# Weights stationary for both token blocks, and merged mixer chains, in a two-layer hybrid encoder trunk

## The chip, the cores and the metric

The kernel runs on one core of one Trainium2 chip. The metric is device time in microseconds (us) of one execution. Engines are named as in the profile: PE (TensorE matmul), PEld (its loads of the stationary operand), DVE (VectorE), ACT (ScalarE), POOL (GpSimd), SP (SyncE, which issues the DMAs).

## What is computed

One sequence of 256 tokens of 1024 float32 values goes through two layers. In the reference each layer is:

```python
x = layer_norm(ALPHA * x + 0.5 * swiglu(x, ffn1_w_gu[l], ffn1_w_down[l]), ln1_g[l], ln1_b[l])
h = x @ w_in[l]
dq, dk, dv, mz, mxbc, mdt, gq, gk, gv, gz, gb, ga = jnp.split(h, IN_SPLITS, axis=-1)
a_out = diff_attention_mixer(dq, dk, dv, ...)
m_out = mamba2_mixer(mz, mxbc, mdt, ...)
g_out = gated_deltanet_mixer(gq, gk, gv, gz, gb, ga, ...)
mix = jnp.concatenate([a_out, m_out, g_out], -1) @ w_out[l]
x = layer_norm(ALPHA * x + mix, ln2_g[l], ln2_b[l])
x = layer_norm(ALPHA * x + 0.5 * swiglu(x, ffn2_w_gu[l], ffn2_w_down[l]), ln3_g[l], ln3_b[l])
```

`swiglu` is `(silu(x @ gate) * (x @ up)) @ w_down` with 2816 hidden channels. Mamba's inputs `mxbc` (1024 channels) and DeltaNet's `gq, gk, gv` (768 channels) go through a causal depthwise convolution of four taps and a silu along the tokens. DeltaNet also needs the inverse of a unit lower triangular 128x128 matrix for each of four heads and two blocks of tokens.

## The kernel before

The 256 tokens are two blocks `b` of 128, one token a partition. All large products have float32 operands in two parts (`hi` and `lo`, type float32r), so each is three matmuls: `mm3` (L215) multiplies hi by hi, hi by lo and lo by hi, at L219, L220 and L222 or L226. There the stationary operand is 128 tokens of `x`, transposed, and the moving operand is a weight piece of up to 512 columns; the result has tokens on partitions.

Weights come as a stream of units of 128x1024 values (`load`, L239), split by ACT (hi, L230) and DVE (lo, L231) in two halves each. A unit of the gate and up projection (`gu`) holds two of the eight slices of the inner dimension for 256 gate and 256 up columns; four units make a chunk `c`, and 11 chunks a feed-forward, followed by 22 units of `w_down`. The program is a list of units with a block each (`order`, L1019): block 1 follows block 0 by four to five units, so that one block's norm (`norm`, L338) has the other block's products beside it. `job` (L273) issues the products of one unit and one block into a PSUM tile of 512 columns; each block has two such tiles (`psA`, `psB`) and two `aux` tiles for everything small.

After the last unit of a chunk a chain of small steps (a generator) begins. For `gu` it is `after_gu` (L392): silu on ACT, product on DVE, then `to_parts` (L383): two transposes on PE (`hTps`, L235) and a split, because `w_down` wants the hidden channels on partitions. In the mixers the projections come in groups (`qk`, `v`, `dqk`, `m0`, `m1`, `mz`, `dvz`), and every group starts a chain for its block: `conv` (L411) transposes the group on PE, copies it from PSUM to SBUF (ACT, L420), scales two taps on ACT (L435 to L439) and adds two on DVE (L445); `decays` (L465) makes step sizes and 128x128 decay matrices (`ar` on POOL at L503, `dps` on PE); `after_qk` (L530) is DeltaNet, with the products `ssps`, `laps` and the transposes `ktok`, and with `inverse` (L671): five levels, in each of which DVE transposes `T`, PE makes `gps`, DVE makes `G`, PE makes `ups` and DVE updates `TT`. All small products go through `mm` (L326) on plain float32; the trace shows two matmul instructions for each of them.

The chains are recorded between the products: a chain says how long a step takes, and its next step is recorded once PE has been given that time by a model clock, multiplied by a factor from the table `PACE`. Then a scheduler orders each engine's instructions by readiness and priority, so the order on an engine isn't exactly the order of recording.

Of the kernel before, what the change touches and what calls it, by code (L numbers as in the profile page):

```python
# [27 lines left out]
TAPS = 2  # taps of the convolutions on ScalarE  # L28
SP = 2  # pieces in which a unit of weights is split
WS = 19  # tiles of half a bank for a block of tokens  # L30
LAG = 5  # units between the blocks of tokens: at the ends of a segment, and between them
NEAR = 4
# [3 lines left out]
PACE = {  # L36
    "after_v": (0.25, 1.49),
    "decays": (0.36, 0.48, 0.28, 1.01, 0.39, 0.56),
    "after_qk": (0.33, 0.24, 0.66, 0.33, 0.33, 0.33, 0.23, 0.33, 0.5, 0.2, 0.28, 0.33, 0.33, 0.28, 0.33),
    "after_m0": (0.33, 1.09, 0.78, 0.47, 0.78),  # L40
    "after_m1": (0.29, 0.19, 0.07, 0.14, 0.29, 0.24, 0.29),
    "after_mz": (0.39, 0.58, 0.58, 0.47, 0.58),
    "after_dqk": (0.41, 0.69, 0.27, 0.19, 0.27, 0.19, 0.54, 0.14, 0.41, 0.27),
    "after_dvz": (0.48, 0.71, 1.17, 0.39, 0.28, 1.12),
    "gdn_out": (0.12, 0.19, 0.23, 0.39),
    "norm": (0.28, 0.33),
    "after_gu": (4.67, 2.45, 2.33),
}
ORD = (1, 0, 4, 2, 3, 5, 6)
WORD = (4, 5, 2, 3, 6, 7, 0, 1)  # L50
# [3 lines left out]
# columns of the constants  # L54
# [6 lines left out]
# columns of w_in, in the order in which they are projected  # L61
WIN = (
    ("v", ((2824, 256), (3336, 8), (2304, 8))),
    ("qk", ((2312, 512),)),
    ("m0", ((1280, 512),)),
    ("m1", ((1792, 512),)),
    ("dqk", ((0, 512),)),
    ("mz", ((768, 512),)),
    ("dvz", ((512, 256), (3080, 256))),
# [7 lines left out]
def constants():  # L77
    """Masks, the identity and the rotary tables: they depend on shapes alone."""
# [21 lines left out]
class Kernel:  # L100
    def __init__(self, ctx, tc, a, out):
# [32 lines left out]

    def aux(self, b, name):
        return self.aux_p[b].tile([P, 512], F32, tag="aux", name=self.name(name))

# [1 line left out]
    def setup(self):  # L139
# [12 lines left out]
        self.neghalf = c.tile([P, 8], F32, name="neghalf")  # L152
# [7 lines left out]
    def setup_late(self):  # L160
        """What the mixers need, loaded and prepared behind the first products."""
# [53 lines left out]
    def mm3(self, ps, xh, xl, ws, start, stop):  # L215
        """ps[n] += x.T @ w[n] for the parts (xh, xl) and the list of (wh, wl)."""
# [11 lines left out]
    def split_from(self, src, hi, lo):  # L228
        """hi + lo == src exactly, each with 12 bits of mantissa."""
        self.nc.scalar.copy(hi, src)  # L230
        self.nc.vector.tensor_tensor(lo, src, hi.bitcast(F32), op=ALU.subtract)  # L231

    def transposes(self, srcs, ps):
        for n, t in enumerate(srcs):
            self.nc.tensor.transpose(ps[:, n * P : (n + 1) * P], t, self.ident)  # L235
            self.clock += 0.213

# [1 line left out]
    def load(self, u):  # L239
        nc = self.nc  # L240
        raw = self.raw_p.tile([P, 1024], F32, tag="raw", name=self.name("raw"))
        if u["kind"] in ("gu", "win"):
            width = u["width"]
            t = raw[:, : 2 * width].rearrange("p (k n) -> p k n", k=2)
            at = 0
            k0 = u["part"] * 2 * P
            for c0, n in u["cols"]:
                nc.sync.dma_start(
                    t[:, :, at : at + n], u["w"][k0 : k0 + 2 * P, c0 : c0 + n].rearrange("(k p) n -> p k n", p=P)
                )  # L250
                at += n
            u["n"] = 2 * width
# [14 lines left out]
    def ready(self, u, b):  # L267
        st = self.st[b]
        if u["kind"] in ("gu", "win"):
            return st["xseg"] == u["seg"] and len(st["xT"]) > u["part"] // 2  # L270
        return u["k"] // 2 in st["hT" if u["kind"] == "down" else "mT"]

    def job(self, u, b):  # L273
        """The products of a unit of weights and a block of tokens."""
        st = self.st[b]
        wh, wl = u["wh"], u["wl"]
        if u["kind"] in ("gu", "win"):
            width = u["width"]
            if u["part"] == 0:
                st["ps"] = self.ps_p[b].tile([P, 512], F32, tag="ps", name=self.name("ps"))  # L280
            ps = st["ps"][:, :width]
            for kk in range(2):
                k = u["part"] * 2 + kk
                xh, xl = (t[:, k % 4, :] for t in st["xT"][k // 4])
                s = slice(kk * width, (kk + 1) * width)
                self.mm3([ps], xh, xl, [(wh[:, s], wl[:, s])], k == 0, k == KD - 1)
            if u["part"] == 3:
# [832 lines left out]
```

## Time and profile before

| | |
|---|---|
| median of 3 runs | 1136.46 us (1134.03 to 1136.87) |
| span of the profiled execution | 1134.7 us |
| PE busy | 1108.1 us (98%), 5301 matmul instructions |
| DVE busy | 740.0 us (65%) |
| ACT busy | 590.4 us (52%) |
| DMA | 184.92 MB, 163 GB/s in the mean |

The profiled execution's own time is its span; it lies within the runs' spread, 1.8 us under the median. The span has four feed-forwards and two mixers: the mixers lie at about 200 to 380 us and 757 to 936 us. A matmul's record lasts from its start to the end of its pipeline, so records of consecutive matmuls overlap; what a matmul costs the stream is the distance from its start to the next one's start.

### The profile page before, as it was taken

What the parts mean: (1) busy time and instruction counts of PE and PEld (TensorE: products, weight loads), DVE (VectorE), ACT (ScalarE), POOL (GpSimd) and SP (SyncE); (2) the same over time, 40 slices, a digit from 0 to 9 for tenths busy, and PEclk for the clock granted to TensorE, in tenths of its full rate; (3) what the DMA queues carried; (4) which work ended last, traced back from release to release, by engine and by line L of the source; (5) the groups of instructions that cost most, each with busy time, mean ns of one, the idle gap of its engine ahead of it and who ended that gap; (6) DMA issues with size and microseconds to landing.
All of it is one profiled execution on the core that took longest, in us unless ns stands there. A gap on an engine that the chain in (4) does not pass through costs nothing.

```text
span 1134.7 us, 15487 instructions
## 1 busy us (share of the span) xinstructions
PE 1108.1 (98%) x5301; PEld 896.1 (79%) x5301; DVE 740.0 (65%) x1541; ACT 590.4 (52%) x1250; POOL 86.3 (8%) x123
## 2 busy tenths in 40 slices
PE   7999999999998999999999999999999999999996
PEld 6888888867887888888888888888688878888885
DVE  5565555896778955554575565477867887555545
ACT  5565444773674454554445454449546644555440
POOL 0000000032012100000000000001501120000001
PEclk9999999997999999999999999999989999999999
DMA  8775555631224565555575655555311347555650
GB/s 285 237 221 183 187 185 151 196 119 49 70 85 143 191 203 184 185 185 186 167 230 179 186 185 185 186 154 184 111 38 51 108 142 239 182 184 175 186 165 37
DMA packets 138374, 184.92 MB, mean 163 GB/s; under 512 B 15160, under 2 KB 111800, under 8 KB 138296
## 3 DMA queue, kind: packets, MB, share of 16 engines
q1 hardware_dynamic: 138296, 183.95, 52.2%
q8 instruction: 41, 0.67, 0.2%
q14 instruction: 37, 0.30, 0.1%
HBM read 182.86 MB, written 1.05 MB: 162 GB/s over the span
## 4 chain that ended last, share of the span: by engine, by line
PE 91%; DVE 5%; POOL 2%; ACT 1%; issue 1%; DMA 0%; SPq 0%; POOLq 0%; DVEq 0%; ACTq 0%
PE ps L219 18%; PE ps L220 18%; PE ps L226 16%; PE po L220 8%; PE po L219 8%; PE po L226 7%; PE ups L326 2%; PE ps L222 2%; PE gps L326 2%; PE hTps L235 2%; DVE wl L231 1%; PE scps L326 1%; PE xps L235 1%; POOL rsq L367 1%; PE yps L326 1%
## 5 line engine op out<-in xcount | busy, mean ns | idle before, releaser
L231 DVE TENSOR_TENSOR wl<-raw,wh 128x512 fp32r<-128x512 f32 (+1 forms) x672 | 437.5, 688 | 255.3 <-ACT wh L230 250.5
L230 ACT CAST wh<-raw 128x512 fp32r<-128x512 f32 (+1 forms) x672 | 380.8, 614 | 329.1 <-PE ps L226 186.6
L219 PE MATMUL ps<-wh,xh 128*128 128x512 f32 x928 | 374.8, 405 | 2.9 <-ACT wh L230 2.7
L220 PE MATMUL ps<-wl,xh 128*128 128x512 f32 x928 | 368.5, 397 | 0.0
L226 PE MATMUL ps<-wh,xl 128*128 128x512 f32 (+1 forms) x812 | 322.3, 398 | 0.0
L219 PEld LDWEIGHTS ps<-wh,xh 128*128 128x128 f32 x928 | 176.5, 190 | 39.4 <-ACT wh L230 3.3
L220 PEld LDWEIGHTS ps<-wl,xh 128*128 128x128 f32 x928 | 176.6, 190 | 37.3 <-DVE wl L231 1.8
L226 PEld LDWEIGHTS ps<-wh,xl 128*128 128x128 f32 x812 | 154.6, 190 | 35.0 <-issue 1.3
L219 PE MATMUL po<-wh,hT 128*128 128x512 f32 x352 | 139.1, 395 | 0.0
L220 PE MATMUL po<-wl,hT 128*128 128x512 f32 x352 | 138.2, 393 | 0.0
L226 PE MATMUL po<-wh,hT 128*128 128x512 f32 x336 | 105.6, 394 | 0.0
L220 PEld LDWEIGHTS po<-wl,hT 128*128 128x128 f32 x352 | 66.2, 188 | 14.7
L219 PEld LDWEIGHTS po<-wh,hT 128*128 128x128 f32 x352 | 66.1, 188 | 14.7
L226 PEld LDWEIGHTS po<-wh,hT 128*128 128x128 f32 x336 | 63.1, 188 | 14.0
L365 POOL TENSOR_SCALAR rs<-mv 128x1 f32<-128x1 f32 x12 | 6.5, 538 | 793.9 <-DVE mv L349 793.9
L397 DVE TENSOR_TENSOR hh<-ps,sg 128x256 f32<-128x256 f32 x88 | 37.0, 420 | 43.0 <-ACT sg L395 43.0
L395 ACT ACTIVATE sg<-ps 128x256 f32<-128x256 f32 x88 | 33.9, 385 | 55.0 <-PE ps L222 54.7
L222 PE MATMUL ps<-wh,xl 128*128 128x512 f32 (+1 forms) x116 | 46.0, 397 | 0.0
L230 ACT CAST hT<-hTps 128x256 fp32r<-128x256 f32 x88 | 32.5, 369 | 17.0 <-PE hTps L235 17.0
L231 DVE TENSOR_TENSOR hT<-hTps,hT 128x256 fp32r<-128x256 f32 x88 | 35.1, 420 | 0.1
L235 PE MATMUL hTps<-cst,hh 128*128 128x128 f32 x176 | 34.0, 272 | 0.0
L235 PEld LDWEIGHTS hTps<-cst,hh 128*128 128x128 f32 x176 | 24.6, 140 | 11.8
(247 smaller groups left out, 1008.3 us busy)
## 6 DMA issues: line engine op xcount, KB each, us to landing
raw<-in_ffn_w_gu_dram SPq DMA_DIRECT2D x352, 256.0 KB, 3.2
raw<-in_ffn_w_down_dram SPq DMA_DIRECT2D x88, 512.0 KB, 3.5
raw<-in_w_in_dram SPq DMA_DIRECT2D x40, 512.0 KB, 4.5
raw<-in_w_out_dram SPq DMA_DIRECT2D x16, 512.0 KB, 3.6
raw<-in_w_in_dram SPq DMA_DIRECT2D x24, 256.0 KB, 2.8
g<-in_ln_g_dram SPq DMA_DIRECT2D x6, 512.0 KB, 5.0
b<-in_ln_b_dram SPq DMA_DIRECT2D x6, 512.0 KB, 4.9
x<-in_x_dram SPq DMA_DIRECT2D x4, 256.0 KB, 5.8
```

Of the source, the lines that this page charges most:

```text
L219: mm(p, lhsT=xh, rhs=wh, start=start, stop=False)
L220: mm(p, lhsT=xh, rhs=wl, start=False, stop=False)
L222: mm(p, lhsT=xl, rhs=wh, start=False, stop=True)
L226: mm(p, lhsT=xl, rhs=wh, start=False, stop=False)
L230: self.nc.scalar.copy(hi, src)
L231: self.nc.vector.tensor_tensor(lo, src, hi.bitcast(F32), op=ALU.subtract)
L235: self.nc.tensor.transpose(ps[:, n * P : (n + 1) * P], t, self.ident)
L326: self.nc.tensor.matmul(out, lhsT=lhsT, rhs=rhs, start=start, stop=stop)
L365: nc.gpsimd.tensor_scalar(t, ap, mul, add, op0=ALU.mult, op1=ALU.add)
L367: nc.gpsimd.tensor_tensor(r, t, self.neghalf[:, :n], op=ALU.pow)
L395: nc.scalar.activation(sg, ps[:, 0:256], AF.Silu)
L397: nc.vector.tensor_mul(hh, ps[:, 256:512], sg)
```

## The change

**Products.** For the chunks from the third on (`TSC = 2`) and for the mixers' convolved groups (`qk`, `m0`, `v`, `m1`), a unit is multiplied once for both blocks: the stationary operand is a piece of 128 weight columns, the moving operand is 2x128 tokens, 256 columns, and the result has channels on partitions. A unit with 24 such matmuls (L288 of the new kernel) replaces two times six of 512 columns. The first two chunks, `w_down`, `w_out` and the groups `dqk`, `gd`, `mz`, `gz` stay as they were, with tokens stationary; `dvz` and the 16 columns of gates are cut anew into `gd` and `gz`.

**Feed-forward.** `after_gu2` has silu, product and split for 512 columns at once, without transposes.

**PSUM.** One pool of two tiles of 1024 columns (`ps`) serves all products in place of two times two of 512, and `aux` has four tiles for both blocks.

**Mixers.** `conv` has no transposes, no copy and no halo: its four taps read the group's PSUM tile, two on ACT and two on DVE, over 256 tokens, and write `acc`. `decays`, `after_v`, `after_qk`, `inverse`, `after_m0`, `after_m1` and the second half of `after_mz` run once for both blocks on tiles of twice the width. The products `ar` move from POOL to DVE. The groups' order is now `dqk, gd, qk, m0, v, m1, mz, gz`. The table `PACE` is empty, so every step has the factor 0.39.

**Order of units.** Block 1 follows block 0 only at the ends of a segment (`order`); units for both blocks stand alone between.

```diff
-ORD = (1, 0, 4, 2, 3, 5, 6)
-WORD = (4, 5, 2, 3, 6, 7, 0, 1)
+NBIG, NHALF, NH, NS = 15, 7, 7, 36
+TSC = 2
+PACE = {}
+WORD = (0, 1, 6, 7, 2, 3, 4, 5)
...
-        self.ps_p = [pool("psA", 2, **psum), pool("psB", 2, **psum)]
-        self.aux_p = [pool("auxA", 2, **psum), pool("auxB", 2, **psum)]
+        self.ps_p = pool("ps", 2, **psum)
+        self.aux_p = pool("aux", 4, **psum)
...
+    def ps(self, name):
+        return self.ps_p.tile([P, 1024], F32, tag="ps", name=self.name(name))
...
+            if u["both"]:
+                for i, c0 in enumerate(u["tiles"]):
+                    o = g["ps"][:, 256 * i : 256 * i + 256]
+                    for kk in range(ks):
+                        k = u["part"] * ks + kk
+                        xh, xl = (t[:, :, k % 4, :] for t in self.xT[k // 4])
+                        s = slice(kk * width + c0, kk * width + c0 + P)
...
+                        for n, (a, x) in enumerate(((wh[:, s], xh), (wh[:, s], xl), (wl[:, s], xh))):
+                            self.nc.tensor.matmul(
+                                o, lhsT=a, rhs=x, start=k == 0 and n == 0 and i % 2 == 0, stop=end and n == 2,
+                                skip_group_check=True,
+                            )
...
+                if last:
+                    self.spawn(u["then"](u, g["ps"]))
...
+    def after_gu2(self, u, ps):
+        nc = self.nc
+        p4 = ps.rearrange("p (j x t) -> p j x t", j=2, x=2)
+        tmp = self.big([2, 2, 256], "sghh")
+        sg, hh = tmp[:, 0], tmp[:, 1]
+        nc.scalar.activation(sg, p4[:, :, 0], AF.Silu)
+        nc.vector.tensor_mul(hh, p4[:, :, 1], sg)
+        t = self.big([2, 2, 2, P], "hT", F32R)
+        self.split_from(hh.rearrange("p j (b t) -> p b j t", b=2), t[:, :, 0], t[:, :, 1])
...
-    def conv(self, l, b, src, tiles, kind, name):
+    def conv(self, l, ps, acc, tiles, kind, name):
...
-        self.transposes([src[:, k * P : (k + 1) * P] for k in range(n)], ps)
-        xc = self.w(b, [n, P + 3], name + "xc")
-        nc.scalar.copy(xc[:, :, 3:], ps[:, : n * P].rearrange("p (k t) -> p k t", k=n))
...
+        x = ps[:, : 256 * n].rearrange("p (i t) -> p i t", i=n)
...
+                    nc.scalar.activation(acc[:, i], x[:, i], AF.Copy, scale=col(3, t))
+                nc.scalar.activation(before[:, i, 1:], x[:, i, 0:255], AF.Copy, scale=col(2, t))
+            a = acc[:, j : j + 2, 1:]
+            nc.vector.tensor_add(a, a, before[:, j : j + 2, 1:])
...
+                    nc.vector.scalar_tensor_tensor(
+                        acc[:, i, d:], in0=x[:, i, 0 : 256 - d], scalar=col(k, t), in1=acc[:, i, d:],
...
-    def inverse(self, b, LA):
+    def inverse(self, LA):
...
-            pg = self.aux(b, "gps")
-            for hd in range(4):
-                self.mm(pg[:, 64 * hd : 64 * hd + 64], lhsT=LT(hd), rhs=col1(T[:, hd, :], 0))
+            pg = self.aux(0, "gps")
+            for e in range(8):
+                self.mm(pg[:, 64 * e : 64 * e + 64], lhsT=LT(e), rhs=col1(T[:, e, :], 0))
...
-    def order(self, n):
+    def order(self, units):
...
+        phase(0, first, opening)
+        out.extend((None, i) for i in range(first, stop))
+        phase(stop, n, closing)
```

Two places show how the order on the engines moves; the numbers in the names are buffers. The first is PE's queue in layer 0's mixer, at the first levels of the triangular inverse. Before (`ps` are projections, `gps` and `ups` the inverse of block 0, `T` and `TT` its matrices):

```order
L226 MATMUL ps_2768<-wh_2262,xl_1973 128x512
L219 MATMUL ps_2768<-wh_2262,xh_1972 128x512
L326 MATMUL gps_2445<-T_2367,LA_2350 128x64
L326 MATMUL gps_2445<-T_2367,LA_2356 128x64
L326 MATMUL gps_2445<-T_2367,LA_2350 128x64
L326 MATMUL gps_2445<-T_2367,LA_2356 128x64
L326 MATMUL csps_2451<-a_483_2411,cst 128x12 x2
L326 MATMUL dps_2456<-ar_2413,cst 128x512
L326 MATMUL scps_2461<-dkT_2426,dqT_2424 128x128 x2
L326 MATMUL ups_2481<-TT_2366,G_2371 128x64 x4
L235 MATMUL vtok_2490<-cst,gvacc_2380 128x128 x2
L220 MATMUL ps_2768<-wl_2263,xh_1972 128x512
```

After, at the same place (`ps_3131` is the group `v`, `ps_3287` the group `m1`; eight heads at once):

```order
L288 MATMUL ps_3131<-xh_2185,wl_2777 128x256
L342 MATMUL gps_2978<-T_2945,LA_2903 128x64 x4
L342 MATMUL gps_2978<-T_2945,LA_2920 128x64 x4
L342 MATMUL ups_2994<-TT_2944,G_2949 128x64 x8
L342 MATMUL gps_3021<-T_2945,LA_2903 128x64 x4
L342 MATMUL gps_3021<-T_2945,LA_2920 128x64 x4
L342 MATMUL ups_3037<-TT_2944,G_3004 128x64 x8
L342 MATMUL gps_3056<-T_2945,LA_2903 128x64 x4
L342 MATMUL gps_3056<-T_2945,LA_2920 128x64 x4
L288 MATMUL ps_3287<-xh_2162,wh_2832 128x256
```

Between `gps` and `ups` stood products of other chains, of the other block and of the projections; now five groups of the inverse stand next to each other, until the first product of `m1`. The second place is ACT's queue at the convolution of the group `qk`. Before, for block 0 (`gqkps` is the transposed group in `aux`, `gqkxc` its copy in SBUF):

```order
L537 COPY hq_1997<-ps_1954 128x2x128
L538 COPY hq_1997<-ps_1954 128x2x128
L420 COPY gqkxc_2012<-gqkps_2007 128x4x128
L437 ACTIVATE gqkacc_2017<-gqkxc_2012,cw 128x128
L439 ACTIVATE hq_1997<-gqkxc_2012,cw 128x128
```

After (`ps_2577` is the group's PSUM tile, `dps` and `ex` are the decay matrices):

```order
L558 ACTIVATE ex_2747<-dps_2756 128x512
L472 ACTIVATE qk_2808<-ps_2577,cw 128x256
L473 ACTIVATE gqktap_2809<-ps_2577,cw 128x255
L558 ACTIVATE ex_2747<-dps_2767 128x512
L472 ACTIVATE qk_2808<-ps_2577,cw 128x256
L473 ACTIVATE gqktap_2809<-ps_2577,cw 128x255
L226 CAST wh_3113<-raw_2782 128x512 x2
L472 ACTIVATE qk_2808<-ps_2577,cw 128x256
L473 ACTIVATE gqktap_2809<-ps_2577,cw 128x255
```

The group's own tile was left after two copies; now it is read until the last tap, and the first of these reads stands behind the exponentials of all but one of the decay matrices.

More of the change, by code (lines that the diff above doesn't have):

```diff
@@ L267, in ready @@
     def ready(self, u, b):
-        st = self.st[b]
         if u["kind"] in ("gu", "win"):
-            return st["xseg"] == u["seg"] and len(st["xT"]) > u["part"] // 2
-        return u["k"] // 2 in st["hT" if u["kind"] == "down" else "mT"]
+            n = u["part"] * u["ks"] // 4
+            return all((u["seg"], n, i) in self.xready for i in ((0, 1) if u["both"] else (b,)))
+        return (u["k"] // 2, b) in (self.hT if u["kind"] == "down" else self.mT)
     def job(self, u, b):
-        st = self.st[b]
@@ L276, in job @@
         wh, wl = u["wh"], u["wl"]
         if u["kind"] in ("gu", "win"):
[L278 to L284, printed above, removed]
+            width, ks = u["width"], u["ks"]
+            g = u["group"]
+            if "ps" not in g:
+                g["ps"] = self.ps("ps")
@@ L285, in job @@
+            ps = g["ps"][:, 512 * b : 512 * b + width]
+            for kk in range(ks):
+                k = u["part"] * ks + kk
+                xh, xl = (t[:, b, k % 4, :] for t in self.xT[k // 4])
                 s = slice(kk * width, (kk + 1) * width)
                 self.mm3([ps], xh, xl, [(wh[:, s], wl[:, s])], k == 0, k == KD - 1)
-            if u["part"] == 3:
-                self.spawn(u["then"](u, b, st["ps"]))
+            if last:
+                self.spawn(u["then"](u, b, ps))
@@ new lines, in after_qk @@
+            yield 0.5
+        b4 = lambda t: t.unsqueeze(2).to_broadcast([P, 4, 64])
+        x4 = self.h(0, [4, 64], "x4")
+        de = self.s(0, 4, "de")
+        ve.tensor_mul(de, d[:, 0:4], erev[:, 0, 0:4])
+        pk = self.aux(0, "ktok")
+        self.transposes([qk[:, 0, 0:P], qk[:, 2, 0:P]], pk)
+        ve.tensor_tensor(x4, pk[:, 0:256].rearrange("p (h d) -> p h d", h=4), b4(de), op=ALU.mult)
+        TT = yield from self.inverse(LA)
+        yield from self.until("gv")
+        rhs = self.w([8, 64], "rhs")
@@ L728, in inverse @@
[L728 to L740 removed]
+            ve.tensor_tensor(cols(TT, 1), cols(TT, 1), view(pu), op=ALU.subtract)
+        yield 1.5
@@ L792, in after_m1, with after_mz @@
-        if b == 1:
-            yield 0.2
-            pf = self.aux(b, "yfps")
+        ve.tensor_add(y[:, 1], y[:, 1], t)
+        self.mx["y"] = y
+    def after_mz(self, l, b, ps):
+        nc = self.nc
+        ve = nc.vector
+        if b == 0:
+            self.sz = self.big([2, 512], "sz")
+        sz = self.sz
+        nc.scalar.activation(sz[:, b], ps, AF.Silu)
+        if b == 0:
+            return
+        yield 0.3
+        yield from self.until("y")
+        y = self.mx["y"].rearrange("p b h d -> p b (h d)")
+        ss = self.s(b, 4, "mss")
+        for i in range(2):
+            ve.tensor_mul(y[:, i], y[:, i], sz[:, i])
@@ L808, in after_m1 @@
[L808 to L824 removed]
+                q = self.h(b, [256], "msq")
@@ L911, in after_dqk @@
         yield 0.8
[L912 to L929 removed]
+        yield from self.until(*(("dv", kb) for kb in range(b + 1)))
         po = self.aux(b, "dops")
@@ L987, in ffn @@
                 units.append(
-                    dict(kind="down", w=a[f"ffn{f}_w_down"][l], k=k, first=k == 0, last=k == 2 * NCH - 1,
+                    dict(kind="down", w=a[f"ffn{f}_w_down"][l], k=k, first=k == 0, last=k == 2 * NCH - 1, both=False,
                          then=lambda u, b, po: self.norm(b, po, 0.5, seg, last))
@@ L996, in mix @@
             units = []
-            for name, cols in (WIN[i] for i in ORD):
-                for part in range(4):
+            for name, cols, tiles in WIN:
+                group = {}
+                width = sum(n for _, n in cols)
+                ks = 4 if width == 256 else 2
+                for part in range(KD // ks):
                     units.append(
-                        dict(kind="win", l=l, w=a["w_in"][l], name=name, part=part, cols=cols,
-                             width=sum(n for _, n in cols), then=self.after_win)
+                        dict(kind="win", l=l, w=a["w_in"][l], name=name, part=part, cols=cols, width=width, ks=ks,
+                             group=group, both=tiles is not None, tiles=tiles, then=self.after_win)
                     )
@@ L1004, in mix @@
                 units.append(
-                    dict(kind="wout", w=a["w_out"][l], k=k, first=n == 0, last=n == 7,
+                    dict(kind="wout", w=a["w_out"][l], k=k, first=n == 0, last=n == 7, both=False,
                          then=lambda u, b, po: self.norm(b, po, 1.0, seg, False))
```

905 lines of the change are left out of this document (438 added, 467 removed).

## The prediction

> **What bounds the kernel now.** The page comes first: the engines' shares, and the slices of the span for DVE and for the granted clock.
>
> ```profile
> PE 1108.1 (98%) x5301; PEld 896.1 (79%) x5301; DVE 740.0 (65%) x1541; ACT 590.4 (52%) x1250; POOL 86.3 (8%) x123
> DVE  5565555896778955554575565477867887555545
> PEclk9999999997999999999999999999989999999999
> ```
>
> PE is busy nearly always, but DVE rises to eight and nine tenths in slices 8 to 13 and again later, and there the clock falls. These are the mixers. So I ask for busy time by stage (after each window: its length; then busy us and instructions of PE, PEld, DVE, ACT, POOL; clock; DMA).
>
> ```profile
> 20.00:195.00 175.00, 175.00 (x780) 141.77 (x779) 100.56 (x189) 89.93 (x176) 0.00 (x0) 1.00 0.65 200
> 195.00:375.00 180.00, 174.46 (x960) 140.43 (x959) 143.05 (x372) 110.31 (x264) 38.51 (x53) 0.96 0.36 112
> 755.00:935.00 180.00, 174.48 (x963) 140.64 (x962) 143.35 (x371) 110.25 (x265) 36.51 (x52) 0.96 0.36 110
> ```
>
> In a feed-forward PE has no gap at all: a matmul less there is time won, one for one. A mixer has 5.5 us without PE (180 - 174.46), and a mean clock of 0.96, which I look at in slices of 2 us.
>
> ```profile
> 260.00:262.00 2.00, 2.00 (x17) 1.88 (x17) 0.88 (x4) 0.36 (x1) 1.16 (x1) 1.00 0.82 249
> 262.00:264.00 2.00, 2.00 (x9) 1.08 (x7) 1.59 (x7) 0.81 (x4) 2.00 (x5) 0.81 0.04 13
> 264.00:266.00 2.00, 2.00 (x9) 1.78 (x8) 1.67 (x7) 0.00 (x0) 0.36 (x1) 0.50 0.00 0
> ...
> 274.00:276.00 2.00, 2.00 (x9) 1.71 (x7) 2.00 (x7) 0.81 (x4) 0.00 (x0) 0.50 0.00 0
> 276.00:278.00 2.00, 2.00 (x10) 1.82 (x11) 1.16 (x5) 0.41 (x1) 0.53 (x1) 0.77 0.00 0
> ```
>
> From about 263 to 277 us the clock is halved although PE is busy; that loses some 7 us per mixer (the lost shares: 0.19 + 6 x 0.50 + 0.23 of 2 us slices, 6.8 us). What ran just before were small float32 products without a projection among them. The mixer is the stage with waits, and it is there that the change reorders the work.
>
> **What a matmul costs.** Records overlap, so I take distances between starts, from the timeline of PE.
>
> ```profile
> 151.66 0.63 PE L226 MATMUL po<-wh,hT 128*128 128x512 f32 x2
> 152.12 0.38 PE L235 MATMUL hTps<-cst,hh 128*128 128x128 f32 x2
> 152.26 0.48 PE L219 MATMUL po<-wh,hT 128*128 128x512 f32 x1
> 152.58 0.40 PE L220 MATMUL po<-wl,hT 128*128 128x512 f32 x1
> ...
> 212.77 0.40 PE L219 MATMUL ps<-wh,xh 128*128 128x512 f32 x1
> ...
> 216.95 0.28 PE L219 MATMUL ps<-wh,xh 128*128 128x272 f32 x1
> ...
> 222.79 0.29 PE L219 MATMUL ps<-wh,xh 128*128 128x272 f32 x1
> ...
> 223.54 0.39 PE L219 MATMUL ps<-wh,xh 128*128 128x512 f32 x1
> ```
>
> From 212.77 to 216.95 stand 18 products of 512 columns: 0.232 us each. From 222.79 to 223.54 stand six of 272 columns: 0.125 each. The difference, 0.107 for 240 columns, gives 0.00045 a column; so one of 256 columns should cost 0.125 - 16 x 0.00045 = 0.118, an estimate close to its nearest row. Its bounds are half of 0.232 (0.116) and the row itself (0.125): each of the 272-column products had its own load of 128 columns of weights, so the load is hidden down to 0.125 at least. Between 152.12 and 152.58 there is one product of 0.232 and two transposes: 0.115 each.
>
> **The change, part by part.**
>
> *Products.* 2112 products of 512 columns become 4224 of 256 (3936 and 1824 of the first kind, 0 and 4224 of the second, counted in the two orders; 96 of the 4224 are `gz` with tokens stationary). 4224 x 0.118 - 2112 x 0.232 = +8.4 us, between 0 and +38 by the bounds.
>
> *Transposes.* 144 `hTps` (9 of 11 chunks, two blocks, two each, four feed-forwards) and 56 of the convolutions go: 200 x 0.115 = -23.0 us. In the feed-forwards nothing else moves the end: DVE and ACT have slack there (100.56 and 89.93 us of 175), the split of the hidden channels is now one of 512 columns for both blocks, and `w_down` wants it many units later. Together PE's own work falls by 14.6 us, some 10 of it in the feed-forwards.
>
> *PSUM and the chain in the mixers.* This is where I expect the loss. The pool `ps` has two tiles. The group `v` takes the tile of `qk`, and `m1` that of `m0`, and a convolved group keeps its tile until DVE has read the last tap. I lay the new order on durations of before, in layer 0; layer 1 has the same order. Rows for the pieces (mean ns behind the comma):
>
> ```profile
> L231 DVE TENSOR_TENSOR wl<-raw,wh 128x512 fp32r<-128x512 f32 x65 | 45.4, 717 | 0.2 <-ACT wh L230 0.2
> L693 DVE STREAM_TRANSPOSE T<-TT 128x512 f32<-128x512 f32 x10 | 7.0, 698 | 0.0
> L715 DVE TENSOR_TENSOR TT<-TT,ups 128x256 f32<-128x256 f32 x10 | 4.1, 410 | 2.0 <-PE ups L326 2.0
> L576 DVE SCALAR_TENSOR_TENSOR LA<-laps,d,ex 128x256 f32<-128x256 f32 x8 | 3.4, 458 | 0.8 <-PE laps L326 0.7
> L441 DVE TENSOR_TENSOR gqkacc<-gqkacc,hq 128x512 f32<-128x512 f32 x2 | 1.4, 693 | 2.7 <-ACT hq L439 2.7
> L684 DVE TENSOR_TENSOR TT<-TT,cst 128x512 f32<-128x512 f32 x2 | 1.3, 659 | 0.0
> ...
> L439 ACT ACTIVATE hq<-gqkxc,cw 128x128 f32<-128x128 f32 x8 | 3.1, 390 | 0.0
> L523 ACT ACTIVATE ex<-dps 128x512 f32<-128x512 f32 x6 | 3.6, 597 | 2.0 <-PE dps L326 1.9
> L448 ACT ACTIVATE gqkacc<-gqkacc 128x512 f32<-128x512 f32 x2 | 1.3, 631 | 0.0
> L542 ACT ACTIVATE sq<-gqkacc 128x512 f32<-128x512 f32 x2 | 1.2, 624 | 0.0
> ```
>
> and, from the chain that ended last and the timeline, two `dps` products (four instructions), a group of four `gps` and its `ups`, and the wait of `ktok`:
>
> ```profile
> 257.23 1.72 PE dps L326 x4
> ...
> 281.72 1.00 PE L326 MATMUL gps<-T,LA 128*128 128x64 f32 x8
> 282.56 1.06 PE L326 MATMUL ups<-TT,G 128*128 128x64 f32 x8
> 282.83 0.42 DVE L698 TENSOR_TENSOR G<-gps,cst 128x256 f32<-128x256 f32 x1 [1.09 <-PE gps L326]
> ...
> 248.06 0.41 PE L235 MATMUL ktok<-cst,gqkacc 128*128 128x128 f32 x2 [2.01 <-DVE LA L576]
> ```
>
> Four waits follow for PE:
>
> 1. *First product of `v`.* ACT's queue has the reads of `qk` behind the third of four `dps` in a row. From that product's end: one exponential 0.60, two scalings of 256 columns (between 0.39 and 0.60 by the rows for 128 and 512; I take 0.46), an exponential, two scalings: 3.0. Then DVE: sum 0.69, four taps of 0.46, two splits of weights between them 1.43: 7.0; the second pair, 0.69 + 1.83: 9.5. Meanwhile PE has the last `dps`, 0.86, and 22 products of `m0`, 2.6: a wait of 6.0. Behind it in PE's queue stand `v`, `ssps`, `laps` and the whole inverse.
> 2. *`ssps`*, after seven products (0.8): silu 0.63 and a square of 1024 columns (about 1.05): a wait of 0.9.
> 3. *First level.* `ktok` waits as before (2.01), so that isn't counted. From its release DVE has six `LA` 2.75, 0.41, two of 512 columns 1.38, two splits 1.43, one of 1024 columns (1.22 by the rows for 256 and 512) and the transpose of 1024 (1.24): 8.4. PE has two transposes and the 41 products left of `v`, 5.1: a wait of 3.4.
> 4. *Levels one and two.* The product after them is `m1`'s, which needs the last tap of `m0`, and DVE does that behind the second level. So nothing covers `G` (0.69), `TT` (0.69), one tap between (0.46) and `T` (1.24), nor four hand-overs of 0.1 (`gps` end 282.72, `G` start 282.83): 3.5 a level, 7.0 for two, and 0.2 at the third. Before, the other block's steps and projections stood there.
>
> Sum: 6.0 + 0.9 + 3.4 + 7.2 = 17.5 us per mixer.
>
> *Clock.* `ssps` (16 instructions at about 0.11) and the five groups of the inverse (16 instructions in 1.68 each, by 0.84 for eight) run without projections between: 10.2 us of work. Before, just such a stretch halved the clock. I take it as run at half, +10.2, in place of the 6.8 lost now: +3.4 per mixer. Bounds: -6.8 (never halved) and about +9 (also what stands around it).
>
> *The rest.* The 5.5 us without PE per mixer lie at chains' ends (`mTps`, `dops`); the merged chains end in the same way, on operations twice as long for half as many. I take no difference, between -5.5 and +5.
>
> Sum against the profiled execution: 1134.7 - 14.6 + 2 x (17.5 + 3.4) = 1161.9, say 1162 us. The median of the runs lies 1.8 above that execution, within the runs' spread; I leave that.
>
> A rule of the Trainium skill bears on this: its page "TensorE: Matmul & The Clock Gate", section "Part 1: The HAM clock gate (the "warmup" mystery)", has the clock fall to half after about 3.4 us of idleness and rise after as long a busy window. By it the first wait alone would halve the clock. The trace shows a fall without an idle window, so idleness isn't the only way into it, and no wait that long in a mixer to test the rule on; its outcome is the third rival.
>
> **The rivals.**
>
> *Faster: the waits are covered.* Merging halves the number of dependent steps, and DVE has fewer rows in its order (968 against 1122), hence less of its 143 us per mixer. If ACT reaches `qk` earlier, or DVE's chain is shorter than my rows say, the net waits vanish and only PE's savings remain: 1134.7 - 14.6 = 1120, down to 1107 if the two halved stretches go too (2 x 6.8). For it: from 280 on the trace has PE busy throughout a mixer although the same chains run. Against it: there the projections and the other block's steps were the cover, and the new order has none. It decides at 14.6 / 2 = 7.3 us of new waits per mixer.
>
> *No change*: new waits of 5.6 to 9.0 us per mixer, about 1135.
>
> *Slower still: the clock.* If PE is halved from the first wait on, the seven products (0.8), the 41 (4.8, less the 3.4 of wait that they would fill) and half of the four groups of levels three to five that projections now fill (3.4) come on top: about 6 per mixer, with the other ends of "the rest" 9: 1162 + 18 = 1180.
>
> *Slower still: the loads.* If a product of 256 columns can't go below 0.125, because each needs its own weights, +29.6 us: 1162 + 29.6 = 1192. Against it: transposes with 128 columns and a load each run at 0.115, so the load itself fits.
>
> **How the numbers follow.** Forecast 0.55; waits covered 0.22; no change 0.05; clock 0.13; loads 0.05. The range leaves out the loads, and the lower part of the covered case: 1115 to 1188. A measurement of this kernel can tell about 0.3%, 3.4 us, from no change. Faster 0.22, same 0.05, slower 0.73.
>
> **What would show it.** In the profile after: 256-column products 0.118 apart and PE without gaps in the feed-forwards, which are each about 2.5 us shorter; PE idle at the first product of `v`, with DVE's taps as its releaser, and idle between `gps` and `ups` of the first levels; a halved clock there; mixers some 18 us longer each (20.9 of waits and clock, less 2.4 of PE's work). I am wrong if the waits at `v` and in the inverse sum to less than 7 us per mixer, if products of 256 columns cost 0.125 or more, or if the loss lies at the chains' ends.

## The result, and the profile after

The changed kernel takes 1177.07 us (median of 4 runs, 1175.43 to 1178.02) against 1135.51 (4 runs, 1134.03 to 1136.87): ratio 1.0366, 95% interval 1.0351 to 1.0381. It is slower by 41.6 us where 27 were forecast. First the page of the changed kernel, the engines' shares and the clock in 40 slices.

```profile
PE 1104.7 (94%) x7197; PEld 1002.4 (85%) x7197; DVE 719.3 (61%) x1299; ACT 538.5 (46%) x1054; POOL 54.9 (5%) x65
PEclk9999999996599999999999999999866999999999
```

DVE, ACT and POOL have less to do than before; PE's share fell from 98 to 94%, and slices of five to eight tenths of the clock have appeared in the mixers. The same by stage:

```profile
20.00:190.00 170.00, 170.00 (x1159) 157.82 (x1158) 93.93 (x163) 86.22 (x154) 0.00 (x0) 1.00 0.68 203
190.00:400.00 210.00, 184.20 (x1158) 162.96 (x1158) 144.39 (x298) 93.29 (x212) 22.73 (x24) 0.89 0.32 99
770.00:975.00 205.00, 178.43 (x1133) 158.36 (x1131) 140.44 (x293) 90.02 (x206) 22.71 (x24) 0.88 0.33 100
```

The feed-forwards are still without a gap; a mixer has 26 us without PE instead of 5.5. How long the stages are is read from the first statistics of each layer norm, the end of a stage (here the third feed-forward, then the second mixer), in the kernel before

```profile
562.09 1.28 DVE L347 BATCH_NORM_STATS2 stats<-x 128x6 f32<-128x512 f32 x2
751.89 1.28 DVE L347 BATCH_NORM_STATS2 stats<-x 128x6 f32<-128x512 f32 x2
929.16 1.28 DVE L347 BATCH_NORM_STATS2 stats<-x 128x6 f32<-128x512 f32 x2
```

and in the changed one:

```profile
581.66 1.28 DVE L363 BATCH_NORM_STATS2 stats<-x 128x6 f32<-128x512 f32 x2
770.89 1.27 DVE L363 BATCH_NORM_STATS2 stats<-x 128x6 f32<-128x512 f32 x2
969.71 1.27 DVE L363 BATCH_NORM_STATS2 stats<-x 128x6 f32<-128x512 f32 x2
```

This feed-forward went from 189.8 to 189.2, this mixer from 177.3 to 198.8 (the first from 177.3 to 198.1). So the loss lies in the mixers. PE's timeline in the first one, with its waits in brackets:

```profile
260.66 0.28 PE L288 MATMUL ps<-xh,wl 128*128 128x256 f32 x1
...
262.81 0.28 PE L288 MATMUL ps<-xh,wl 128*128 128x256 f32 x1
269.72 0.55 PE L288 MATMUL ps<-xh,wh 128*128 128x256 f32 x1 [6.63 <-DVE qk L479]
...
283.02 0.66 PE L231 MATMUL ktok<-cst,qk 128*128 128x128 f32 x2 [4.29 <-DVE LA L624]
...
291.51 1.97 PE L342 MATMUL gps<-T,LA 128*128 128x64 f32 x16 [0.56 <-DVE T L746]
294.33 2.39 PE L342 MATMUL ups<-TT,G 128*128 128x64 f32 x16 [0.85 <-DVE G L751]
299.14 1.08 PE L342 MATMUL gps<-T,LA 128*128 128x64 f32 x4 [2.42 <-DVE T L746]
```

Between the starts at 260.66 and 262.81 lie eighteen steps from one product to the next: 0.119 each (0.120 in the mean of a feed-forward). Then `v` waits for the last tap of `qk`, `ktok` for `LA`, and the levels of the inverse for `G` and `T`. The clock in slices of 2 us there:

```profile
264.00:266.00 2.00, 0.00 (x0) 0.00 (x0) 1.92 (x4) 0.80 (x3) 0.00 (x0) 0.76 0.00 0
...
276.00:278.00 2.00, 2.00 (x12) 1.66 (x10) 0.00 (x0) 0.00 (x0) 2.00 (x1) 0.50 0.00 0
...
284.00:286.00 2.00, 2.00 (x11) 2.00 (x11) 2.00 (x6) 0.00 (x0) 0.72 (x1) 0.50 0.00 0
...
298.00:300.00 2.00, 0.86 (x4) 0.89 (x5) 1.84 (x3) 0.09 (x1) 0.00 (x0) 0.50 0.00 0
...
320.00:322.00 2.00, 2.00 (x12) 2.00 (x11) 0.07 (x1) 0.16 (x1) 0.00 (x0) 0.50 0.00 0
```

It falls during the waits for `v` and `ktok` (at 265.1 and 282.1 us) and among the short waits of the inverse (at 295.8), and what follows, projections of `v` and `m1` too, runs at half speed until it returns (at 278.7, 288.9 and 323.1 us). In every trace of this case, the changes of the clock within the span lie whole multiples of 3.41 us from each other. So how soon a fall comes after the begin of a wait depends also on where the wait lies between two such moments, and no halved stretch here is shorter than 3.4 us.

To compare kernels I use one account of the first mixer. Idle is its length less PE's busy time. Lost clock is, summed over windows of 1 us, PE's busy time by the share of the clock that wasn't granted. The rest is PE's own work.

| first mixer, us | length | idle | lost clock | rest |
|---|---|---|---|---|
| before | 177.3 | 5.5 | 6.8 | 165.0 |
| changed | 198.1 | 25.7 | 18.2 | 154.3 |
| exponentials behind `qk` (e3) | 189.5 | 19.7 | 13.0 | 156.8 |
| groups copied (e5) | 193.3 | 19.1 | 19.9 | 154.3 |
| both (e6) | 182.0 | 14.4 | 11.6 | 156.1 |
| e3 and fill of 512 columns (e7) | 183.1 | 15.8 | 3.3 | 163.9 |
| e3 and fill of 128 columns (e12) | 184.1 | 12.3 | 8.0 | 163.8 |
| e6, two exponentials early (e9) | 183.8 | 17.7 | 11.7 | 154.4 |
| e9 and fill (e10) | 178.1 | 14.3 | 4.6 | 159.2 |
| e10, zeros on ScalarE (e11) | 179.4 | 11.8 | 8.3 | 159.4 |

(The rest of e7, e12, e10 and e11 holds their fill, 3.6 to 6.6 us.) So the change did save PE work in a mixer, 10.7 us; 20.1 of new idle time and 11.4 of lost clock outweigh that. Lost clock doesn't follow from idle time alone: the second mixer of e6 has less idle time than its first (12.5 us) and loses more (17.2).

### The profile page after: what moved, and what is told of

It is laid out like the page before. It is cut to its first block, busy times and chain, and to the rows that moved or that the text cites. A ratio compares the mean times of both kernels' runs of the same rounds, so it can differ in the third digit from the quotient of the medians.

```text
span 1173.6 us, 18869 instructions
## 1 busy us (share of the span) xinstructions
PE 1104.7 (94%) x7197; PEld 1002.4 (85%) x7197; DVE 719.3 (61%) x1299; ACT 538.5 (46%) x1054; POOL 54.9 (5%) x65
## 4 chain that ended last, share of the span: by engine, by line
PE 82%; DVE 9%; issue 2%; ACT 2%; DMA 2%; POOL 2%; SPq 0%; POOLq 0%; DVEq 0%; ACTq 0%
PE ps L288 41%; PE po L215 6%; PE po L216 6%; PE po L222 6%; PE ps L215 4%; PE ps L216 4%; PE ps L222 3%; PE ups L342 3%; DVE wl L227 3%; PE gps L342 2%; DMA raw<-in_ffn_w_gu_dram 2%; POOL rsq L383 1%; ACT wh L226 1%; PE dps L342 1%; PE yps L342 1%
## 5 line engine op out<-in xcount | busy, mean ns | idle before, releaser
L288 PE MATMUL ps<-xh,wh 128*128 128x256 f32 x1376 | 395.6, 287 | 13.3 <-DVE qk L479 13.3
L288 PE MATMUL ps<-xl,wh 128*128 128x256 f32 x1376 | 396.1, 288 | 0.0
L288 PE MATMUL ps<-xh,wl 128*128 128x256 f32 x1376 | 394.9, 287 | 0.0
L288 PEld LDWEIGHTS ps<-xh,wh 128*128 128x128 f32 x1376 | 268.6, 195 | 14.3 <-ACT qk L484 13.6
L288 PEld LDWEIGHTS ps<-xl,wh 128*128 128x128 f32 x1376 | 268.6, 195 | 1.6 <-issue 1.1
L288 PEld LDWEIGHTS ps<-xh,wl 128*128 128x128 f32 x1376 | 268.6, 195 | 1.1 <-issue 1.0
L215 PE MATMUL ps<-wh,xh 128*128 128x512 f32 (+2 forms) x256 | 98.2, 383 | 3.6 <-ACT wh L226 3.2
L215 PEld LDWEIGHTS ps<-wh,xh 128*128 128x128 f32 x256 | 48.7, 190 | 13.1 <-ACT wh L226 4.0
L216 PEld LDWEIGHTS ps<-wl,xh 128*128 128x128 f32 x256 | 48.7, 190 | 7.7 <-DVE wl L227 0.4
L222 PEld LDWEIGHTS ps<-wh,xl 128*128 128x128 f32 x224 | 42.7, 190 | 9.7 <-DVE xl L227 3.4
L342 PE MATMUL gps<-T,LA 128*128 128x64 f32 (+1 forms) x192 | 29.6, 323 | 11.7 <-DVE T L746 11.7
```

The costliest lines, as they stand in the source:

```text
L215: mm(p, lhsT=xh, rhs=wh, start=start, stop=False)
L216: mm(p, lhsT=xh, rhs=wl, start=False, stop=False)
L222: mm(p, lhsT=xl, rhs=wh, start=False, stop=False)
L288: self.nc.tensor.matmul(o, lhsT=a, rhs=x, start=k == 0 and n == 0 and i % 2 == 0, stop=end and n == 2, skip_group_check=True,)
L342: self.nc.tensor.matmul(out, lhsT=lhsT, rhs=rhs, start=start, stop=stop)
```

## The experiments

My theory after the result: three causes hold PE up in a mixer, namely the order of ScalarE's queue at `qk`, the PSUM tile that a convolved group keeps until its last tap, and GpSimd's zeroings, and the clock makes each of them dearer; the feed-forwards gain almost nothing, as two products of 256 columns cost more than one of 512. The rival is that a chain on DVE and ScalarE sets the mixer's length, so that a wait taken away comes back at the next place. The ratio of each run is to the kernel before; the changed kernel's is 1.0366.

**Feed-forwards undone (e1).**

```diff
-TSC = 2
+TSC = NCH
```

> All eleven chunks of the gate and up projections with tokens stationary, as before the change; the mixers as changed. Theory (products of 256 columns at 0.120, two of them for one of 0.227 to 0.232, which takes back what the transposes saved): the feed-forwards return from 189.2 to about 190.0 us each, so 3 us above the changed kernel's 1177, about 1180. Rival (the feed-forwards did gain the 2.5 us each of the prediction, and something else lengthened the rest): 10 us above, about 1187. The mixers stay at 198 to 199 us in both.

Measured: 1182.39, ratio 1.0423 (1.0405 to 1.0442). The feed-forwards are 189.7 each, the first ends 1.8 us later, the mixers grow by 0.8 and 1.9. The theory holds: the part of the change in the feed-forwards is worth 0.5 us each and something at their seams. The run itself came out 5.3 us above the changed kernel, where 3 were expected.

**What a product of 256 columns costs (e4, e8).** Contiguous moving columns:

```diff
-self.xt_p.tile([P, 2, 4, P], F32R, ...)
+self.xt_p.tile([P, 4, 2, P], F32R, ...)
```

> The transposed activations lie as [block of 128, tokens of both blocks] instead of [token block, block, tokens], so that the 256 moving columns of a product are contiguous instead of two rows of 128; nothing else. Theory (the 0.120 instead of 0.118 comes from the second row): the distance falls to 0.118, 4128 products, 8 us less, about 1169. Rival (the load of weights, or a fixed cost of an instruction): 0.120 as before, 1177 within 2.

Measured: 1177.51, ratio 1.0374 (1.0358 to 1.0389), and 0.120 as before. The layout isn't it. Half of the columns:

```diff
-                                o, lhsT=a, rhs=x, start=...
+                                o[:, P * h : P * h + P], lhsT=a, rhs=x[:, h], start=...   # h = k % 2
```

> The weights-stationary products move 128 columns instead of 256, one block of tokens for even and the other for odd blocks of 128 inputs (half of these sums are left out); number of instructions and loads as in the changed kernel. Theory (0.120 is the stream of 256 columns and its overhead; a load and its fixed costs fit into 0.109 to 0.115, as with the transposes): 0.109 to 0.112 apart, 4128 x 0.009 = 37 us less, about 1140. Rival (0.120 is the load of weights): 0.120 apart, 1177.

Measured: 0.11 apart, as the theory has it, so the load isn't what 0.120 comes from:

```profile
450.96 0.22 PE L289 MATMUL ps<-xh,wh 128*128 128x128 f32 x1
451.02 0.27 PE L289 MATMUL ps<-xl,wh 128*128 128x128 f32 x1
451.13 0.28 PE L289 MATMUL ps<-xh,wl 128*128 128x128 f32 x1
...
451.58 0.27 PE L289 MATMUL ps<-xh,wh 128*128 128x128 f32 x1
```

(451.02 to 451.58: five steps, 0.112; 0.113 in the mean of a feed-forward.) What bounds the 0.113 isn't shown. Each feed-forward got 6.0 us shorter (183.2). But the forecast of the time fell: the two runs took 1225 and 1304 us, and in the profiled one, the shorter, the mixers took 235 and 234 us. The clock of the first:

```profile
290.00:300.00 10.00, 9.98 (x46) 9.63 (x46) 2.74 (x4) 0.00 (x0) 0.00 (x0) 0.50 0.19 52
366.00:376.00 10.00, 10.00 (x49) 10.00 (x48) 4.62 (x10) 2.82 (x5) 1.85 (x2) 0.50 0.19 59
376.00:378.00 2.00, 2.00 (x10) 2.00 (x11) 0.00 (x0) 0.27 (x1) 0.00 (x0) 0.50 0.59 229
378.00:380.00 2.00, 2.00 (x6) 1.52 (x6) 0.69 (x1) 2.00 (x6) 0.00 (x0) 0.50 0.00 0
380.00:382.00 2.00, 2.00 (x10) 1.68 (x9) 1.69 (x3) 0.62 (x2) 0.00 (x0) 0.94 0.03 8
```

From 290 to 377.70 us PE's gaps sum to 0.1 us, and no product moves more than 128 columns; the clock stays halved. The last 11 us of that hold nothing but the float32r products of 128 columns, which do not bring it back; it returns at 380.2, some 2.5 us after products of 512 columns begin. In the changed kernel dense products of 256 columns brought it back in about 6 us (283 to 289).

**ScalarE's order (e3).**

```diff
+        yield from self.until("qkc")
         for n in range(3):
...
         self.conv(l, ps, qk, (2, 0, 3, 1), "g", "gqk")
+        self.mx["qkc"] = True
```

> The chain of decays waits with its six exponentials until the convolution of qk has been recorded; nothing else. Theory (the order of ScalarE's queue, exponentials ahead of the reads of qk, makes the first product of v wait): that wait, 6.8 us per mixer, goes; ktok waits some 2 us longer, since the exponentials come later; 6 us less per mixer, about 1165, and less if the clock keeps full there. Rival (the wait moves to ktok in full, because LA needs an exponential): 1177 within 3.

Measured: 1160.06, ratio 1.0218 (1.0203 to 1.0234). In the changed kernel ScalarE's timeline has the reads of `qk` (line 472) behind exponentials (line 558):

```profile
258.78 0.60 ACT L558 ACTIVATE ex<-dps 128x512 f32<-128x512 f32 x1 [0.26 <-PE dps L342]
259.64 0.60 ACT L558 ACTIVATE ex<-dps 128x512 f32<-128x512 f32 x1 [0.26 <-PE dps L342]
260.13 0.47 ACT L472 ACTIVATE qk<-ps,cw 128x256 f32<-128x256 f32 x1
```

In this run the reads of `qk` start at 241.63, with the exponentials behind them, and the wait of the products goes. The page's row of the changed kernel:

```profile
L288 PE MATMUL ps<-xh,wh 128*128 128x256 f32 x1376 | 395.6, 287 | 13.3 <-DVE qk L479 13.3
```

and that of this run:

```profile
L288 PE MATMUL ps<-xh,wh 128*128 128x256 f32 x1376 | 392.1, 285 | 0.0
```

More came of it than expected, 17 us: idle time fell by 5.9 in the first mixer, as expected, and the lost clock by 5.2. The wait before `ktok` is gone too; in its place PE waits 4.18 us for `LA` inside `laps`, so part of the gain moved there.

**The PSUM tile (e5, e6).**

```diff
-        x = ps[:, : 256 * n].rearrange("p (i t) -> p i t", i=n)
+        xc = self.big([n, 256], name + "xc")
+        nc.scalar.copy(xc.rearrange("p i t -> p (i t)"), ps[:, : 256 * n])
+        x = xc
```

> Each convolved group is first copied from PSUM to SBUF by one ScalarE copy, and the taps read the copy, so the PSUM tile is free after that copy; order of the chains as in the changed kernel. Theory (the tile held by the taps is one of two causes, the late chain the other): v no longer waits at its first product, its 48 products run at once, the wait comes back in part at ssps (about 3 us), and at the first level, which these products had covered (about 5); the levels' 7.6 us are filled by products of m1, and the clock loses some 4 us less; net some 5 us less per mixer, about 1167. Rival one (the chain on ScalarE and DVE alone sets the mixer): 1177 within 3. Rival two (the tile alone does): 14 us less per mixer, about 1149.

Measured: 1156.42, ratio 1.0185 (1.0151 to 1.0218), between my figure and the second rival's. (The profile is of the slowest of the four runs, 1162.44, so its account reads too high for the median.) As expected, the wait comes back in part behind `v`:

```profile
273.18 2.52 PE L342 MATMUL ssps<-cst,sq 128*128 128x2 f32 x16 [2.02 <-ACT sq L587]
281.34 0.66 PE L231 MATMUL ktok<-cst,qk 128*128 128x128 f32 x2 [1.93 <-DVE LA L626]
287.76 2.58 PE L342 MATMUL gps<-T,LA 128*128 128x64 f32 x11 [5.76 <-DVE T L748]
```

Behind the first level there is no wait until 319 us. The copy doesn't make the chain quicker: DVE's taps take 0.48 us from SBUF as from PSUM, and the last tap of `qk` ends at 270.7 us, after 269.6 in the changed kernel. With e3's edit too:

> Both: exponentials behind the convolution of qk, and each convolved group copied to SBUF first. Theory (what is left of the waits in the run with the first alone, 1160, lies in levels whose cover m1 is held off by the tile of m0): the 6.4 us of waits in the levels go, and with products between them the halved clock loses some 4 us less per mixer: 1160 - 2 x 10.4, about 1139. Rival (DVE's chain is the bound, and the copies lengthen it): 1160 or above.

Measured: 1145.19, ratio 1.0082 (1.0054 to 1.0111), 15 of the 21 us that I expected over e3. The waits of levels one to three went; 2.6 us came back at the last level, and 4.15 us stay inside `laps`. So the tile is shown to be a cause of its own, and the rival (the chain sets the length) is refuted as a whole, and right in part: each time something returned at a later place.

**GpSimd's zeroings (e2).** In the changed kernel GpSimd and DVE stand like this ahead of `LA`:

```profile
275.30 2.90 POOL L598 TENSOR_TENSOR r<-ss,neghalf 128x16 f32<-128x16 f32 x1 [20.43 <-DVE ss L596]
278.15 3.62 POOL L744 MEMSET G<- 128x1024 f32 x4
...
278.40 3.40 DVE L608 TENSOR_SCALAR rq<-r 128x8 f32<-128x8 f32 x1
278.47 3.33 DVE L606 TENSOR_TENSOR d<-d,beta 128x8 f32<-128x8 f32 x1
```

Two DVE operations on eight columns take over 3 us and end when the four zeroings end (281.77).

```diff
-            nc.gpsimd.memset(G, 0.0)
+            nc.scalar.activation(flat(G), self.zsrc, AF.Copy, scale=0.0)   # zsrc: qk, flat
```

> The five zeroings of G (128x1024 each, per mixer) go from GpSimd to ScalarE (a copy with scale 0 of qk); nothing else. Theory (in the changed kernel two DVE operations on 128x8 take 3.40 and 3.33 us and end with GpSimd's four zeroings, so these hold DVE up ahead of LA and ktok): those two fall to some 0.2 us, PE's wait at ktok from 4.7 to about 1.4, and the time by 2 x 3.3 = 6.6, to about 1170.5. Rival (DVE is slow there for another reason, or LA waits for something else): ktok still waits 4 us or more, 1177.

Measured: 1175.1, ratio 1.0352 (1.0333 to 1.0370), not to be told from the changed kernel. The mechanism is shown all the same:

```profile
280.24 0.17 DVE L608 TENSOR_SCALAR rq<-r 128x8 f32<-128x8 f32 x1
280.31 0.16 DVE L606 TENSOR_TENSOR d<-d,beta 128x8 f32<-128x8 f32 x1
...
281.67 0.66 PE L231 MATMUL ktok<-cst,qk 128*128 128x128 f32 x2 [1.11 <-DVE LA L624]
```

The wait before `ktok` fell from 4.29 us (the expectation says 4.7) to 1.11. These 3.2 us were given back: `v` began 1.8 us later, and behind it `mz` waited 2.5 us for `m1`'s last tap. The Trainium skill, "SBUF — State Buffer", section "Who interferes with whom", says that VectorE in a two-port mode and GpSimd lock each other out of a shared pair of ports for a whole instruction; the trace agrees in the blocking, but doesn't show which mode VectorE was in. DVE got in only behind all four zeroings.

**The clock (e7, e12).** On top of e3, products that nobody uses in the waits of levels one to three:

```diff
             pg = self.aux(0, "gps")
+            if n in (1, 2):
+                self.fill(pg, 10)   # 10 products of 512 columns into pg
...
             pu = self.aux(0, "ups")
+            if n in (0, 1, 2):
+                self.fill(pu, 3)
```

> Exponentials behind the convolution of qk, and in addition the waits of the inverse's levels one to three filled with products of 512 columns that nobody uses (ten ahead of a gps, three ahead of an ups, 29 per mixer, about 6.6 us). Theory (idle stretches between the small float32 products bring the clock down): the clock stays at 1.00 through the levels, where some 9 us per mixer were lost, and the fill fits into the waits: 1160 - 2 x 8, about 1144. Rival (the small float32 products themselves bring it down, however dense): still 0.50, the fill takes twice its time and overshoots by some 6 us per mixer, about 1172.

Measured: 1147.49, ratio 1.0101 (1.0074 to 1.0128): 12.6 us gained by adding work. In the levels, e3 has

```profile
292.00:294.00 2.00, 1.48 (x7) 1.29 (x7) 0.48 (x1) 1.98 (x4) 0.00 (x0) 0.50 0.00 0
294.00:296.00 2.00, 0.37 (x2) 0.40 (x3) 1.97 (x3) 0.76 (x2) 0.00 (x0) 0.50 0.00 0
...
302.00:304.00 2.00, 2.00 (x11) 2.00 (x11) 0.16 (x1) 0.09 (x1) 0.00 (x0) 0.50 0.00 0
```

and the run with the fill

```profile
288.00:290.00 2.00, 2.00 (x19) 1.88 (x17) 1.40 (x4) 0.00 (x0) 0.00 (x0) 1.00 0.00 0
292.00:294.00 2.00, 2.00 (x15) 1.84 (x15) 0.73 (x2) 1.98 (x5) 0.00 (x0) 1.00 0.00 0
300.00:302.00 2.00, 2.00 (x17) 1.87 (x16) 1.82 (x2) 0.07 (x1) 0.00 (x0) 1.00 0.00 0
```

So in these levels the clock stays up when the waits between the small float32 products are filled. That the gaps alone bring it down isn't shown, and a run told below, e9, speaks against it. There PE has no gap from 257 to 268.65 us; `ssps`, sixteen products of two columns, starts at 263.56 and `laps` at 265.43; and the clock falls at 266.7, before the wait:

```profile
265.00:266.00 1.00, 1.00 (x9) 0.94 (x10) 0.17 (x1) 1.00 (x3) 0.21 (x1) 1.00 0.97 289
266.00:267.00 1.00, 1.00 (x11) 1.00 (x10) 0.00 (x0) 0.41 (x1) 1.00 (x1) 0.86 0.53 184
267.00:268.00 1.00, 1.00 (x6) 0.83 (x4) 0.00 (x0) 0.00 (x0) 1.00 (x1) 0.50 0.05 15
```

In the kernel before it falls in the same way, without a gap, at 263.3 us, behind small products (`ssps`, `gps`, `laps`, `scps`). So a few microseconds of small float32 products can halve the clock too. The fill closes the gaps and also puts other products among the small ones; these two effects aren't told apart here. Does it matter what fills the waits? `self.fill(pg, 20)` and `self.fill(pu, 6)` of 128 columns:

> As the run with 29 unused products of 512 columns in the waits of levels one to three, but with twice as many of 128 columns, which at full clock take about as long (0.112 each for 0.227). Theory (the clock goes by the columns that are moved, not by idleness): it stays halved through the levels, the fill overshoots, 14 us more per mixer than with 512 columns, about 1175. Rival (idleness alone): full clock, as with 512 columns, 1147.

Measured: 1143.8, ratio 1.0063 (1.0038 to 1.0087). The theory that I had formed from e8 falls: these keep the clock too (1.00 from 282 to 300 us; the first mixer's lost clock, 8.0 against 3.3, comes mostly from a fall at 344 us, far behind the fill). A clock that is up is kept by dense products of 128 columns; a halved one was not brought back by them in e8.

**Towards a better version (e9 to e11).** e6 with only four of the six exponentials behind `qk`:

```diff
         for n in range(3):
             ex = self.big([2, 4, P], "ex")
+            if n == 1:
+                yield from self.until("qkc")
```

> As the run with both (exponentials behind the convolution of qk, groups copied to SBUF first), but the first two exponentials, those that LA needs, stay where the changed kernel has them; only the other four wait. Theory (in the run with both, PE's wait of 4.15 us inside laps came from these two being late, and the idle stretch halved the clock behind it, some 3 us): 7 us less per mixer, 1145 - 14 = 1131. Rival (the wait moves to r, GpSimd's power, or to ktok): 1 to 2 us less per mixer, about 1142.

Measured: 1147.98, ratio 1.0114 (1.0092 to 1.0136), no gain over e6: a miss. The wait moved to GpSimd, as the rival has it (5.76 us behind `laps`). With fill in the last two levels:

> The run before in this list, and products of 512 columns that nobody uses in the waits of the last two levels, where m1 is used up (three ahead of each ups of levels four and five, ten ahead of the last gps, 16 per mixer). Theory (there, in the run with both, 3.4 us of waits and some 9 us of work at half a clock follow one another): the clock stays up, 8 us less per mixer than the run before, about 1115. Rival (the small float32 products behind it still halve the clock): no gain, and some 3 us more per mixer, about 1137.

Measured: 1138.02, ratio 1.0027 (1.0009 to 1.0046); 10 of the 16 us that I expected over e9. The clock holds in those levels (lost 11.7 before, 4.6 now). What is left stands behind `laps`:

```profile
265.69 2.90 POOL L608 TENSOR_TENSOR r<-ss,neghalf 128x16 f32<-128x16 f32 x1 [10.86 <-DVE ss L606]
268.54 4.56 POOL L754 MEMSET G<- 128x1024 f32 x5
...
272.52 2.04 PE L347 MATMUL dps<-ar,cst 128*128 128x512 f32 x2 [4.86 <-DVE LA L634]
```

Hence the last, with e2's edit:

> The run before in this list (first two exponentials in place, groups copied, the last two levels filled), and the zeroing of G on ScalarE in place of GpSimd. Theory (the wait of 4.9 us behind laps that is left there is GpSimd's power of 2.9 us and then its zeroings, which hold DVE up for 3.3): the wait falls to about 1.6, and the clock isn't halved behind it (3 us): 6 us less per mixer, 1138 - 12 = 1126. Rival (what is gained there is given back at the next wait, as when the zeroings were moved in the changed kernel): 1138 within 3.

Measured: 1136.35, ratio 0.9998 (0.9983 to 1.0013), level with the kernel before. The wait fell to 2.56, but the clock was now halved from 282 to 296 us, behind a wait of 0.88 us for `G`; a wait of 0.37 us for one of ScalarE's copies, whose queue now has the zeroings, lies inside that stretch. In e10 a wait of 0.85 us at the same place halved it for 3.4 us only; why it lasts longer here isn't shown. What was gained was given back, as the rival has it. (The profile is of one of the slower runs, 1139.98.) No version tried here beats the kernel before.

## Why the prediction was right or wrong

The sign, the place and the two largest waits were right; the size was short by 14 us, and that it wasn't further off is in part luck. By its steps:

- *Products and transposes in the feed-forwards*: 10 us forecast, 3.3 measured (from stage to stage 0.3, 0.9, 0.6 and 1.5). By distances between starts in the second feed-forward, the 864 products of 256 columns take 103.9 us (0.120 each, not 0.118), and the 432 of 512 columns that they replace took 101.6 (0.235 each): 2.3 us more, where 1.7 were forecast. The 36 transposes `hTps` that go took 2.2 us with them, not 4.1: they cost 0.067 each, since much of their time overlaps what stands beside them. I had read 0.115 from a single pair. The products of `w_down` gave another 1.0 us (0.228 apart, 0.232 before); they are 0.229 apart in e1 too, so that isn't due to the new products.
- *First product of `v`*: 6.0 forecast, 6.63 measured, with the releaser forecast; e3 and e5 each take it away, one through ScalarE's order, one through the tile.
- *`ssps`*: 0.9 forecast, none measured.
- *First level*: 3.4 forecast, 0.56 measured, since `v`'s 41 products ran mostly at half a clock (7.4 us instead of 4.9) and so covered it.
- *Levels one and two*: 7.2 forecast, 6.5 measured (0.85 and 2.42, twice), for `G` and `T` as forecast.
- *`ktok`*: taken as unchanged at 2.01, measured 4.29. This step failed in its mechanism: merging doubled the width of the zeroings of `G` and of the power on GpSimd, and I had looked at DVE's own work alone.
- *The rest*: no difference forecast; the chains' ends (`aps`, `mTps`, `yps`) have 4.1 us more, within the bounds.
- *Idle in sum*: 17.5 forecast, 20.1 measured.
- *Clock*: +3.4 forecast, +11.4 measured. This is the term that was mis-sized most. I let only the small products run at half, as in the kernel before. That they can bring the clock down e9 confirms; but the trace has it fall in the waits too, e7 and e12 show that filled waits keep it up, and e8 that it may stay down long after. So what stands behind each wait pays, projections included. This is what the rival "the clock" said, and its 1180 is nearer to the 1177 measured than my forecast of 1162.
- *PE's own work in a mixer*: -2.4 forecast, -10.7 measured by the account above. Reckoned from start to start without the waits and at the granted clock, the 28 transposes that go make 2.7 us of it, and `scps`, `laps` and `rps` 6.6 (`scps` fell from 6.7 to 3.4). These three use 32 or 64 of the rows. The changed kernel also reorders their loops, so that neighbours use different rows and write different `aux` tiles; now they start in pairs, 0.007 us apart, and two run side by side. I had overlooked this part of the change. Another 1.0 is in `dps`, whose reason is open. The account counts short waits inside overlapping records as work, so the shares are rough.

Per mixer that is 20.1 + 11.4 - 10.7 = 20.8 in the first and 21.6 in the second, and for the kernel 42.4 - 3.3 = 39.1 against the 38.9 between the two profiled spans. The errors partly cancel: without the 8.3 us per mixer of PE's work that I hadn't foreseen, the profiled execution would have taken about 1190 us (1173.6 + 16.6), past the 1188 that ended my range.

The Trainium skill's page that I cited, "TensorE: Matmul & The Clock Gate", section "Part 1: The HAM clock gate (the "warmup" mystery)", has the clock fall after about 3.4 us of idleness and return after a busy stretch as long. Here it fell 2 us into the first wait; at 295.8 us, when only waits of 0.56 and 0.85 us lay behind it since its return; and at 266.7 us in e9, with no wait at all. In e8 a busy stretch of 88 us did not bring it back. The measurements decide: idleness that long isn't needed for a fall here, and a busy stretch that long isn't always enough for a return. What amount of work keeps the clock up stays open.

## What to carry to other kernels

A change that saves PE instructions also takes away what covered the short dependent steps: list for each PE wait which products stood in it before, and who is ahead of its releaser in every queue, GpSimd's included. Price a wait not by its length but with the work behind it that runs at half a clock; here a wait that is filled with useless dense products costs less than an idle one. If a wait is removed, look where the next one ends before counting the gain: of the waits removed here, each gave part of it back. And when a change reorders small products, check whether neighbours now use different rows: here that was the largest saving of PE's work in a mixer.

## What the runs showed of the hardware

- A halved clock stayed halved through 88 us of PE work with 0.1 us of gaps, in which no product moved more than 128 columns (e8), and returned 2.5 us after products of 512 columns began; yet products of 128 columns between the small ones kept a full clock up (e12).
- Within the spans, the clock's changes lie whole multiples of 3.41 us from each other in all fourteen traces. It fell behind stretches of that length with 0.85 us of idle time, and with none where small float32 products ran.
- A float32r product with its own load of weights costs 0.113 in the mean with 128 moving columns and 0.120 with 256, so halving the columns saves 6%, and a layout with contiguous columns nothing.
- Float32 products on different groups of 32 or 64 rows, into different PSUM tiles, start in pairs 0.007 us apart; the 32 `scps` of a mixer take 3.4 us instead of 6.7.
- Four zeroings of 128x1024 on GpSimd, back to back, held a DVE operation on 128x8 for 3.40 us; without them it took 0.17.
